# Attention scores with a second key tile for each head

## The chip, the cores and the metric

The kernel runs on one core of a Trainium2 chip. The metric is the device time of one execution in microseconds (us). TensorE is called PE, and its loads of stationary operands are shown apart as PEld; VectorE is DVE, ScalarE is ACT, GpSimd is POOL, and SyncE (SP) issues most of the DMAs.

## The reference

The program is a chain of layers over 256 latent and 256 context tokens of 1024 features: two hybrid layers (feed-forward, attention, feed-forward), then a mixer, a feed-forward, a second mixer and a last feed-forward. What the change touches is the attention of the two hybrid layers. It has 12 heads of 64 features in two groups of six; heads are handled in pairs. Cut to the scores:

```python
HEAD_DIM = 64
def gqa_attention(q, k, v):            # first group of heads
    s = einsum('bqhgd,bkhd->bhgqk', qi, k).astype(float32) * dh ** -0.5
    p = softmax(s, axis=-1)
    return einsum('bhgqk,bkhd->bqhgd', p, v)
def neighbourhood_attention(q, k, v, k_ctx, v_ctx, rpb, rows):   # second group
    s_win = einsum('bqhd,brqjhd->bhqrj', qr, kw) * scale + bias
    s_ctx = einsum('bqhd,bkhd->bhqk', qr, k_ctx) * scale
    p = softmax(concatenate([s_win, s_ctx]), axis=-1)
```

All of it is in float32. The kernel keeps that precision by splitting each operand into two float32r parts, a high part and the low rest, and by adding products of parts: high times high, high times low, low times high.

## The kernel before

A tile has 128 partitions (rows). A matmul contracts over rows, so a product with full precision takes three matmuls of 128 rows (mm3, lines 169 to 174, stationary weights, called pj where it is a projection). For scores a head has only 64 features, and the kernel packs both parts into the 128 rows. `queries` (lines 733 to 742) writes for each head a tile q[a] with the high part of the queries on the head's own 64 rows and the low part on the other 64. `keys` (lines 726 to 731) writes for a pair of heads three tiles: k[0] and k[1] hold the high part of one head's keys twice, on both halves, and k[2] holds the low parts of both heads, each on its own 64 rows. In `scores` (lines 671 to 689) each head then takes two matmuls into one PSUM bank: line 680 contracts all 128 rows of q[a] and k[a] (high times high plus low times high), and line 681 contracts only the 64 rows of the head (high times low).

Scores are taken for 128 queries at a time. In the first hybrid layer there are 6 pairs of heads by 4 tiles of queries by 2 heads, 48 in all: 24 against 512 keys, 24 (the context's queries) against 256. In the second only the latent's queries are left: 24 against 512 keys. So line 681 runs 72 times.

Around the scores: DVE takes the maximum of each row (line 685), ACT the exponents (line 687), and two steps later the generator `values` transposes the exponents on PE (line 699) and multiplies them by the values (line 708). Between these steps `fill` puts the remaining projections (the generator `others`, lines 758 to 808), three matmuls for each chunk of weights, so that PE has work while a softmax runs. Weights arrive by SP's DMAs as raw tiles; ACT writes the high part (line 115) and DVE, at a few places POOL, the low part (line 116). The order of instructions on each engine is fixed when the program is built: a scheduler places them by their dependences and by its own estimate of durations. Each engine works its list in that order. Chunk tiles (tag "ck", 54 of 128 x 512 in pool p1) are shared by the keys, queries, exponents and activations of a stage; a slot is used again when its last reader is done.

Of the kernel before, what the change touches and what calls it, by code (L numbers as in the profile page):

```python
# [6 lines left out]
F32 = mybir.dt.float32  # L7
# [8 lines left out]
# columns of the packed per-feature vectors  # L16
# [42 lines left out]
# order of the modulation's chunks: shift and scale of a norm side by side  # L59
# [7 lines left out]
class Weights:  # L67
    """Weight tiles of 128 columns in the order of use, split into two float32r parts."""
# [52 lines left out]
    def go_on(self, aside):  # L121
        """Splits on after a pause."""
        if self.held:
            self.held = False
            self.aside = aside
            while self.split_at <= min((self.pos - 1) // TPB + self.B.LOOK, self.nb - 1):
                self._split(False)
# [12 lines left out]
    def to(self, b):  # L140
        """Splits the blocks before b."""
        while self.split_at < min(b, self.nb):
            self._split()


class Builder:
# [22 lines left out]
    def mm3(self, ps, w, x, first, last):  # L169
        """Weights stationary."""  # L170
        mm = self.nc.tensor.matmul
        mm(ps, w[0], x[0], start=first, stop=False)  # L172
        mm(ps, w[0], x[1], start=False, stop=False)  # L173
        mm(ps, w[1], x[0], start=False, stop=last)  # L174

    def mm3t(self, ps, x, w, first, last):
        """Activations stationary."""
        mm = self.nc.tensor.matmul
        mm(ps, x[0], w[0], start=first, stop=False)  # L179
        mm(ps, x[0], w[1], start=False, stop=False)  # L180
        mm(ps, x[1], w[0], start=False, stop=last)  # L181
# [33 lines left out]
    def split(self, pool, src, w, tag, name, bufs=None, hi="act", lo="dve"):  # L215
        """Two float32r parts of src."""
        p = self.parts(pool, w, tag, name, bufs)
        if hi == "act":
            self.act(p[0], src)
        else:  # L220
            self.cp(p[0], src)
        (self.tt if lo == "dve" else self.gt)(p[1], src, p[0].bitcast(F32), ALU.subtract)
        return p

    def scaled(self, parts, p, scale, o):
        """Two float32r parts of p times a column."""
        self.act(parts[0][:, o], p[:, o], scale=scale)
        self.stt(parts[1][:, o], p[:, o], scale, parts[0][:, o].bitcast(F32), ALU.mult, ALU.subtract)
# [8 lines left out]
    def rstd(self, src, n, shape, bias=None):  # L237
        """1/sqrt(src/n + eps) of a small tile."""
        t = self.sml.tile(shape, F32, tag="rs%d" % shape[1], bufs=4, name="rs")
        self.act(t, src, ACTF.Sqrt, scale=1.0 / n, bias=self.eps[:shape[0], :] if bias is None else bias)  # L240
        self.nc.vector.reciprocal(t, t)
        return t

    def preload(self, func, dep):
        """Makes the scalar engine load the table of func once dep is there."""
        t = self.sml.tile([128, 1], F32, tag="pl", name="pl")
        self.act(t, dep, func, scale=0.0, bias=self.eps)
# [6 lines left out]
    def new_ss(self):  # L254
        """Place of a sum of squares."""
        return self.sml.tile([128, 1], F32, tag="ss1", bufs=16, name="ss")

    def half_bias(self, ss):
        """Half of the mean square of 1024 features, plus eps."""
        b = self.sml.tile([128, 1], F32, tag="bi", bufs=8, name="bi")  # L260
        self.ts(b, ss, 1.0 / 1024, 1e-6, ALU.mult, ALU.add)
        return b

    def rms_rows(self, h, both=False):
        """Reciprocal root mean square of 1024 features of 128 tokens, by one engine or both."""
        ss = [self.new_ss() for _ in range(2)]
        self.sq(h[:, 0:512], ss[0])
        b = self.half_bias(ss[0])
        if both:
            j = self.tmp.tile([128, 512], F32, tag="jv", bufs=1, name="jv")  # L270
            self.nc.vector.scalar_tensor_tensor(out=j, in0=h[:, 512:1024], scalar=1.0, in1=h[:, 512:1024],
                                                op0=ALU.mult, op1=ALU.mult, accum_out=ss[1])
        else:
            self.sq(h[:, 512:1024], ss[1])
        return self.rstd(ss[1], 1024.0, [128, 1], bias=b)

    def normed(self, pool, t):
        """Place of the normed rows of 128 tokens."""
# [20 lines left out]
    def pre(self, pool, T, A, shift, by=None, need=None, urgent=0):  # L299
        """Normed, scaled and transposed h: yields the 8 chunks of two parts, of by tiles of 128 tokens  # L300
        first and then of the next ones."""
# [46 lines left out]
    def follow(self, nxt):  # L348
        """The norm of layer and place nxt starts within the last product before it."""
# [6 lines left out]
    def gain_rows(self, rows):  # L356
        """Halves of gains on all partitions: [128, 2, 512]."""
# [25 lines left out]
    def out_rest(self, yg, ss, t, both):  # L383
        """Adds the normed product of 128 tokens to h."""
# [11 lines left out]
    def out_half(self, pool, ps, xs, i, G, yg, ss, tail):  # L396
        """Product of the chunks xs with half of the next weights by token; in the second half the tokens
        end one tile after the other."""
# [23 lines left out]
    def out_main(self, po, xs, n, places):  # L422
        """Product of the first chunks with the next weights, of 256 tokens; the last weights' places."""
# [13 lines left out]
    def out_tail(self, pool, po, xs, G, before=None):  # L437
        """The last 4 chunks, one tile of tokens after the other."""
# [30 lines left out]
    def halves(self):  # L469
        """Place of a block of weights in the chunks' slots."""  # L470
        return self.p1, 512, ("ck", "ck"), {}

    def fourth(self):
        """Place of a block of weights that stays until the first one of block 2's next product."""
        return self.up, TPB * 128, ("w4", "w4"), {"bufs": 2}

    def out512(self, pool, xs, G):
        """Product of the chunks xs with the next weights by token, normed and added to h."""
# [7 lines left out]
    def group(self, us, n, T, halves=False):  # L486
        """The first n products, one chunk of us after the other; their banks and the chunks."""
# [15 lines left out]
    def group256(self, us, place):  # L503
        """The first 4 products of 256 tokens, by token and one tile of tokens after the other."""
# [32 lines left out]
    def proj_tm(self, u, nt):  # L537
        """Token-major product with the next 8 groups of 4 weight tiles: one bank for each 128 tokens."""
# [8 lines left out]
    def ada_loads(self):  # L547
        """Loads the modulation's first weights and, between them, those of the first product."""
# [10 lines left out]
    def ada_pe(self, m):  # L559
        """A pair of chunks on the tensor engine, four parts of the contraction side by side."""  # L560
# [15 lines left out]
    def c_rows(self):  # L576
        """The conditions on all partitions."""
# [8 lines left out]
    def ada_dve(self, m):  # L586
        """A pair of chunks on the vector engine, columns on partitions."""
# [14 lines left out]
    def ada(self, n):  # L602
        """The next n pairs of chunks of 128 columns of the modulation's product."""
# [67 lines left out]
    def scores(self, pool, q, kz, t, bias):  # L671
        """Exponents of two heads' scores of 128 queries, and their sums."""
# [4 lines left out]
        for a in range(2):  # L677
            ps = self.psum("sc")
            o, r = slice(t * 128, (t + 1) * 128), slice(64 * a, 64 * a + 64)
            nc.tensor.matmul(ps[:, :nk], q[a][:, o], kz[a][:, k0:], start=True, stop=False)  # L680
            nc.tensor.matmul(ps[:, :nk], q[a][r, o], kz[2][r, k0:], start=False, stop=True)  # L681
# [9 lines left out]
    def values(self, pool, r, vt, vc, o):  # L691
        """Weighted values of two heads by token, in two steps."""
# [20 lines left out]
    def attn(self, l, last, end, nxt=None):  # L713
# [4 lines left out]
        if l == 0:  # L718
# [3 lines left out]
        # the first parts of each head's keys twice, and the second parts of both heads  # L722
        kz = [[pool.tile([128, 512], F32R, tag="ck", name="kz") for a in range(3)]
              for i in range(3)]

        def keys(k, x):
            for a in range(2):
# [3 lines left out]
                self.tt(k[2][r, :], x[r, :], k[a][r, :].bitcast(F32), ALU.subtract)  # L731

        def queries(x, scale=1.0):
            """Both parts of each head's queries, the first on the rows of its head."""
# [12 lines left out]
        # values, token-major  # L747
# [5 lines left out]
        # the other products run between the steps of the attention  # L753
# [60 lines left out]
        # keys and queries of the first group, normed by head and rotated  # L814
# [135 lines left out]
    def to_features(self, tms, gain, c, x, t0=0):  # L950
        """Transposes chunk c of token-major tiles to two parts, times a gain."""
# [6 lines left out]
    def decay(self, pool, X, Y, mask):  # L958
        """exp(min(X_l + Y_s, mask)) for four heads: [s, head, l]."""
# [10 lines left out]
    def log1p_exp(self, pool, x, shape):  # L970
        """log(1 + exp(-|x|))."""
# [9 lines left out]
    def mixer0(self):  # L981
        nc, tc = self.nc, self.tc
        MUL, ADD, SUB, MIN, MAX = ALU.mult, ALU.add, ALU.subtract, ALU.min, ALU.max
        with tc.tile_pool(name="mx0", bufs=1) as sp, tc.tile_pool(name="mck", bufs=16) as ck:
# [6 lines left out]
            # step sizes and gates  # L991
# [18 lines left out]
            # [t, dir, 16 + 8]  # L1010
# [20 lines left out]
            # running maxima, on rows of heads  # L1031
# [38 lines left out]
            # convolved channels: 8-11 are the groups' B and C  # L1070
# [17 lines left out]
            # keys by token of the chunk that passes a state on: dir 0 from chunk 0, dir 1 from chunk 1  # L1088
# [91 lines left out]
            # gate z, states between the chunks, and the skip  # L1180
# [208 lines left out]
    def mixer1(self):  # L1389
        nc, tc = self.nc, self.tc  # L1390
        MUL, ADD, SUB, MIN, MAX = ALU.mult, ALU.add, ALU.subtract, ALU.min, ALU.max
        with tc.tile_pool(name="mx1", bufs=1) as pool, tc.tile_pool(name="gck", bufs=16) as ck:
# [16 lines left out]
            # cumulated logarithms of the gates  # L1409
# [240 lines left out]
def weight_tiles(np, I):  # L1650
    """Tiles of 128 rows and 128 columns, in the order in which the program takes them."""
# [95 lines left out]
def host_arrays(np, I):  # L1747
# [38 lines left out]
    # rotation tables  # L1786
# [17 lines left out]
    # position bias with the window's bounds: [head, row in tile, query column, row offset, key column]  # L1804
# [44 lines left out]
```

## Time and profile before

| what | value |
|---|---|
| time, median of 3 runs | 2654.98 us (2650.44 to 2655.12) |
| span of the profiled execution | 2645.6 us; the profile gives no other time for it |
| PE busy | 2561.1 us, 97% of the span |
| DVE busy | 1749.5 us, 66% |
| ACT busy | 1157.4 us, 44% |
| POOL busy | 196.5 us, 7% |
| chain that ended last | PE 89%, DVE 6%, ACT 2% |

The span runs from the first to the last instruction of the profiled execution; the metric also counts what lies around it. Matmuls are pipelined: the record of one lasts longer than the step from its start to the next one's start. A row of PE that is fully busy is therefore not yet PE at its best pace, and the steps between starts tell the pace.

### The profile page before, as it was taken

The page shows a single profiled execution, that of the slowest core. Times are in us where ns is not written, and L with a number is a line of the kernel's source. Part 1 is how long each engine was busy: PE and PEld are TensorE (multiplying, and loading weights), DVE is VectorE, ACT ScalarE, POOL GpSimd, SP SyncE. Part 2 cuts the span into 40 slices and gives each one's busy share as a digit, 9 for nine tenths or more (in the row PEclk, how much of TensorE's full clock was granted, in tenths as well). Part 3 has the DMA queues.
Part 4 walks back from the last instruction along what each step waited for, and adds up shares of the span by engine and source line. Part 5 has one row for each costly group of instructions (what it writes and reads, how often), then busy time and mean ns, then how long its engine had stood idle before and what let it go on. Part 6 is the DMA issues. An engine that isn't in the chain of part 4 may idle for free.

```text
span 2645.6 us, 36990 instructions
## 1 busy us (share of the span) xinstructions
PE 2561.1 (97%) x13876; PEld 2142.5 (81%) x13876; DVE 1749.5 (66%) x3538; ACT 1157.4 (44%) x1994; POOL 196.5 (7%) x117
## 2 busy tenths in 40 slices
PE   6999999999999999999999999999999899999998
PEld 3888888777888887888888787997977799776997
DVE  4899435555899424898325666557767787666884
ACT  2322234444422224322224545445646566465663
POOL 2000000000000000000000101002352200121000
PEclk9999999999999999999999999999999999999999
DMA  6566331211366323565222313554434355534454
GB/s 251 183 221 220 116 122 66 72 38 58 128 222 219 102 92 104 169 220 193 96 88 86 110 62 121 185 188 151 149 128 131 108 183 184 164 123 136 147 183 157
DMA packets 124740, 375.52 MB, mean 142 GB/s; under 512 B 13840, under 2 KB 15504, under 8 KB 124304
## 3 DMA queue, kind: packets, MB, share of 16 engines
q1 hardware_dynamic: 123408, 369.22, 42.6%
q10 hardware_dynamic: 1152, 3.94, 0.4%
q8 instruction: 109, 1.79, 0.3%
q14 instruction: 71, 0.58, 0.1%
HBM read 372.05 MB, written 1.05 MB: 141 GB/s over the span
## 4 chain that ended last, share of the span: by engine, by line
PE 89%; DVE 6%; ACT 2%; issue 1%; DMA 1%; POOL 1%; SPq 0%; DVEq 0%; ACTq 0%; POOLq 0%
PE pj L172 15%; PE pj L174 15%; PE pj L173 15%; PE po L179 8%; PE po L181 8%; PE po L180 8%; PE pv L708 2%; PE tm L180 1%; PE tm L179 1%; PE tm L181 1%; PE gp L173 1%; PE gp L172 1%; PE gp L174 1%; DVE w L116 1%; PE sc L681 1%
## 5 line engine op out<-in xcount | busy, mean ns | idle before, releaser
L115 ACT ACTIVATE w<-raw 128x1024 fp32r<-128x1024 f32 (+1 forms) x564 | 572.3, 1022 | 977.1 <-PE pj L173 338.4
L116 DVE TENSOR_TENSOR w<-raw,w 128x1024 fp32r<-128x1024 f32 (+1 forms) x533 | 628.2, 1186 | 475.2 <-ACT w L115 467.8
L172 PE MATMUL pj<-uh,w 128*128 128x256 f32 (+1 forms) x2376 | 800.7, 337 | 2.1 <-ACT P L190 2.1
L174 PE MATMUL pj<-uh,w 128*128 128x256 f32 (+1 forms) x2376 | 794.2, 334 | 0.0
L173 PE MATMUL pj<-ul,w 128*128 128x256 f32 (+1 forms) x2376 | 793.7, 334 | 0.0
L172 PEld LDWEIGHTS pj<-uh,w 128*128 128x128 f32 x2376 | 451.6, 190 | 55.0 <-issue 5.3
L174 PEld LDWEIGHTS pj<-uh,w 128*128 128x128 f32 x2376 | 451.7, 190 | 48.1 <-issue 0.6
L173 PEld LDWEIGHTS pj<-ul,w 128*128 128x128 f32 x2376 | 451.8, 190 | 46.0
L597 DVE SCALAR_TENSOR_TENSOR aj<-adaw,cB 128x512 f32<-128x512 f32 x512 | 360.9, 705 | 9.5 <-DMA adaw<-in_wada 1.0
L179 PE MATMUL po<-w,sh 128*128 128x512 f32 x792 | 312.7, 395 | 0.0
L181 PE MATMUL po<-w,sl 128*128 128x512 f32 x792 | 311.9, 394 | 0.0
L180 PE MATMUL po<-w,sh 128*128 128x512 f32 x792 | 311.3, 393 | 0.0
L116 POOL TENSOR_TENSOR w<-raw,w 128x1024 fp32r<-128x1024 f32 (+1 forms) x46 | 111.6, 2425 | 1489.1 <-ACT w L115 1473.5
L181 PEld LDWEIGHTS po<-w,sl 128*128 128x128 f32 x792 | 149.0, 188 | 33.7
L179 PEld LDWEIGHTS po<-w,sh 128*128 128x128 f32 x792 | 148.9, 188 | 33.8 <-DVE yg L193 0.6
L180 PEld LDWEIGHTS po<-w,sh 128*128 128x128 f32 x792 | 148.9, 188 | 33.7 <-DVE w L116 0.7
L179 PE MATMUL tm<-w,uh 128*128 128x512 f32 x224 | 91.0, 408 | 0.0
L180 PE MATMUL tm<-w,uh 128*128 128x512 f32 x224 | 89.3, 399 | 0.6 <-POOL w L116 0.5
L193 DVE TENSOR_TENSOR sg<-sg,pj 128x512 f32<-128x512 f32 (+1 forms) x82 | 50.8, 620 | 58.1 <-PE pj L174 57.9
L181 PE MATMUL tm<-w,ul 128*128 128x512 f32 x224 | 89.1, 398 | 0.0
L190 ACT ACTIVATE ux<-tr,mod,Am 128x256 f32<-128x256 f32 (+1 forms) x96 | 49.7, 545 | 72.5 <-PE tr L327 29.2
L327 PE MATMUL tr<-cst,hn 128*128 128x128 f32 x240 | 52.4, 301 | 28.4 <-DVE hn L203 25.9
(339 smaller groups left out, 3153.2 us busy)
## 6 DMA issues: line engine op xcount, KB each, us to landing
raw<-in_w SPq DMA_DIRECT2D x554, 512.0 KB, 3.3
adaw<-in_wada SPq DMA_DIRECT2D x288, 256.0 KB, 3.2
bt<-in_bias SPq DMA_DIRECT2D x12, 192.0 KB, 2.4
hl<-in_x ACTq DMA_DIRECT2D x1, 1024.0 KB, 8.3
hc<-in_x ACTq DMA_DIRECT2D x1, 1024.0 KB, 8.6
gc<-in_gcst ACTq DMA_DIRECT2D x1, 512.0 KB, 3.6
out<-hl SPq DMA_DIRECT2D x2, 256.0 KB, 2.2
out<-hl ACTq DMA_DIRECT2D x2, 256.0 KB, 2.3
```

The costliest lines, as they stand in the source:

```text
L115: nc.scalar.activation(out=hi, in_=ri, func=ACTF.Copy)
L116: eng.tensor_tensor(out=lo, in0=ri, in1=hi.bitcast(F32), op=ALU.subtract)
L172: mm(ps, w[0], x[0], start=first, stop=False)
L173: mm(ps, w[0], x[1], start=False, stop=False)
L174: mm(ps, w[1], x[0], start=False, stop=last)
L179: mm(ps, x[0], w[0], start=first, stop=False)
L180: mm(ps, x[0], w[1], start=False, stop=False)
L181: mm(ps, x[1], w[0], start=False, stop=last)
L193: self.nc.vector.tensor_tensor(out=out, in0=a, in1=b, op=op)
L327: nc.tensor.transpose(p[:, t * 128:(t + 1) * 128], hn[t][c // 4][:, (c % 4) * 128:(c % 4 + 1) * 128], self.ident)
L597: nc.vector.scalar_tensor_tensor(out=x, in0=w, scalar=1.0, in1=self.cB[:, s, i * 512:(i + 1) * 512], op0=ALU.mult, op1=ALU.mult, accum_out ...
L708: nc.tensor.matmul(po[:, a * 64:a * 64 + 64], x[:, kt * 128:(kt + 1) * 128], vt[k0 + kt][:, vc + a * 64:vc + a * 64 + 64], start=kt == 0, ...
```

## The change

The low part of the keys gets a tile for each head: k[2] and k[3] instead of k[2] alone. Each holds the low part on the head's own 64 rows and zeros on the other 64, which six instructions on POOL for each attention write at its start. Line 681 now contracts all 128 rows: the zeros meet the low part of the queries and add nothing. The number of matmuls is the same. (The diff also takes comments and docstrings out, and the lines below 721 move down by three.)

```diff
@@ scores
-            o, r = slice(t * 128, (t + 1) * 128), slice(64 * a, 64 * a + 64)
+            o = slice(t * 128, (t + 1) * 128)
             nc.tensor.matmul(ps[:, :nk], q[a][:, o], kz[a][:, k0:], start=True, stop=False)
-            nc.tensor.matmul(ps[:, :nk], q[a][r, o], kz[2][r, k0:], start=False, stop=True)
+            nc.tensor.matmul(ps[:, :nk], q[a][:, o], kz[2 + a][:, k0:], start=False, stop=True)
@@ attn
-        kz = [[pool.tile([128, 512], F32R, tag="ck", name="kz") for a in range(3)]
+        kz = [[pool.tile([128, 512], F32R, tag="ck", name="kz") for a in range(4)]
               for i in range(3)]
+        for k in kz:
+            for a in range(2):
+                nc.gpsimd.memset(k[2 + a][64 - 64 * a:128 - 64 * a, :].bitcast(F32), 0.0)
 
         def keys(k, x):
             for a in range(2):
                 r, o = slice(64 * a, 64 * a + 64), slice(64 - 64 * a, 128 - 64 * a)
                 self.act(k[a][r, :], x[r, :])
                 self.cp(k[a][o, :], x[r, :])
-                self.tt(k[2][r, :], x[r, :], k[a][r, :].bitcast(F32), ALU.subtract)
+                self.tt(k[2 + a][r, :], x[r, :], k[a][r, :].bitcast(F32), ALU.subtract)
```

Since the two heads' low parts no longer share a tile, the scheduler also places some instructions otherwise. SP's list is unchanged, and PE's is unchanged up to the second attention. Two places follow.

On POOL, from the start of the program to the second attention; w is a block of weights, rt and qk belong to the rotation of queries and keys. Before:

```order
L113 TENSOR_TENSOR w<-raw,zero 128x1024
L116 TENSOR_TENSOR w<-raw,w 128x1024 x3
L196 TENSOR_TENSOR rt<-qk,ac 128x256 x2
L196 TENSOR_TENSOR qk<-rt 128x256 x2
L116 TENSOR_TENSOR w<-raw,w 128x1024 x6
```

And now:

```order
L113 TENSOR_TENSOR w<-raw,zero 128x1024
L116 TENSOR_TENSOR w<-raw,w 128x1024
L727 MEMSET kz 64x512 x6
L116 TENSOR_TENSOR w<-raw,w 128x1024 x2
L196 TENSOR_TENSOR rt<-qk,ac 128x256 x2
L196 TENSOR_TENSOR qk<-rt 128x256 x2
L116 TENSOR_TENSOR w<-raw,w 128x1024 x4
L727 MEMSET kz 64x512 x6
L116 TENSOR_TENSOR w<-raw,w 128x1024 x2
```

The six writes of zeros stand before the two splits of weights that POOL takes over at the start of each attention, and those splits queue behind them.

On DVE at the start of the second attention, from the keys' low parts to the first queries' low parts (qs<-qk); the first scores on PE wait for that last row. Before:

```order
L193 TENSOR_TENSOR kz<-qk,kz 64x512
L116 TENSOR_TENSOR w<-raw,w 128x1024
L241 RECIPROCAL rs<-rs 128x4
L199 SCALAR_TENSOR_TENSOR qk<-qk,g_12177,hb 128x256
L193 TENSOR_TENSOR rt<-rot,ac 128x256
L208 COPY rr<-rs 128x256
L193 TENSOR_TENSOR qk<-rt 128x256
L199 SCALAR_TENSOR_TENSOR qk<-qk,g_12177,hb 128x256
L193 TENSOR_TENSOR rt<-rot,ac 128x256
L116 TENSOR_TENSOR w<-raw,w 128x1024
L199 SCALAR_TENSOR_TENSOR qs<-qk,qs 64x256 x2
```

And now:

```order
L193 TENSOR_TENSOR kz<-qk,kz 64x512 x2
L241 RECIPROCAL rs<-rs 128x4
L199 SCALAR_TENSOR_TENSOR qk<-qk,g_12186,hb 128x256
L193 TENSOR_TENSOR rt<-rot,ac 128x256
L208 COPY rr<-rs 128x256
L116 TENSOR_TENSOR w<-raw,w 128x1024
L193 TENSOR_TENSOR qk<-rt 128x256
L199 SCALAR_TENSOR_TENSOR qk<-qk,g_12186,hb 128x256
L193 TENSOR_TENSOR rt<-rot,ac 128x256
L199 SCALAR_TENSOR_TENSOR qs<-qk,qs 64x256 x2
```

The split of weights that stood straight before qs<-qk stands four rows earlier, and a split fewer lies between the keys and the queries. On PE the sums, the transpose and the rotation that feed these rows come 14 projection matmuls earlier than before (measured on the list of PE, from 6240 to 6226), and one of the two last rotations comes one group of projections after the other.

## Rows read from the trace of the kernel before

**Rows 1.** The page's part on the chain that ended last, by engine.
```profile
PE 89%; DVE 6%; ACT 2%; issue 1%; DMA 1%; POOL 1%; SPq 0%; DVEq 0%; ACTq 0%; POOLq 0%
```

**Rows 2.** Busy time by stretch: PE, PEld, DVE, ACT, POOL, clock, DMA.
```profile
500.00:560.00 60.00, 60.00 (x308) 45.87 (x308) 32.07 (x63) 29.66 (x66) 1.68 (x1) 1.00 0.14 45
560.00:625.00 65.00, 63.53 (x371) 49.29 (x370) 40.97 (x93) 29.91 (x76) 0.00 (x0) 1.00 0.12 39
1540.00:1600.00 60.00, 58.62 (x377) 48.14 (x376) 34.51 (x72) 27.97 (x61) 0.00 (x0) 1.00 0.16 51
```

**Rows 3.** Line 681 by shape: count, busy us, mean ns, idle before.
```profile
L681 PE MATMUL sc<-kz,qs 64*128 64x512 f32 x48 | 23.5, 509 | 0.2 <-DVE kz L193 0.2
L681 PE MATMUL sc<-kz,qs 64*128 64x256 f32 x24 | 9.1, 381 | 0.0
```

**Rows 4.** Timeline of PE around one score: start, us, line, shape, count.
```profile
505.91 0.40 PE L174 MATMUL pj<-uh,w 128*128 128x512 f32 x1
506.14 0.40 PE L680 MATMUL sc<-kz,qs 128*128 128x512 f32 x1
506.47 0.50 PE L681 MATMUL sc<-kz,qs 64*128 64x512 f32 x1
506.90 0.50 PE L172 MATMUL pj<-uh,w 128*128 128x512 f32 x1
507.24 0.40 PE L173 MATMUL pj<-ul,w 128*128 128x512 f32 x1
```

**Rows 5.** The loads of the same score; in brackets the idle before.
```profile
506.47 0.18 PEld L681 LDWEIGHTS sc<-kz,qs 64*128 64x128 f32 x1 [0.37 <-issue]
506.90 0.19 PEld L172 LDWEIGHTS pj<-uh,w 128*128 128x128 f32 x1 [0.25 <-issue]
```

**Rows 6.** Timeline of PE: first and last of two scores against 256 keys.
```profile
510.65 0.28 PE L680 MATMUL sc<-kz,qs 128*128 128x256 f32 x1
...
512.13 0.39 PE L173 MATMUL pj<-ul,w 128*128 128x512 f32 x1
```

**Rows 7.** Timeline of PE at the start of the second attention.
```profile
1504.70 0.79 PE L680 MATMUL sc<-kz,qs 128*128 128x512 f32 x1 [2.05 <-DVE qs L199]
...
1507.60 0.58 PE L172 MATMUL pj<-uh,w 128*128 128x256 f32 x1
...
1511.67 0.28 PE L173 MATMUL pj<-ul,w 128*128 128x256 f32 x1
1511.79 0.28 PE L174 MATMUL pj<-uh,w 128*128 128x256 f32 x1
...
1512.28 0.40 PE L680 MATMUL sc<-kz,qs 128*128 128x512 f32 x1
...
1516.04 0.39 PE L172 MATMUL pj<-uh,w 128*128 128x256 f32 x1 [2.09 <-ACT P L190]
```

**Rows 8.** Busy time by stretch, as in rows 2: five us after that start.
```profile
1505.00:1510.00 5.00, 5.00 (x15) 3.26 (x15) 4.47 (x11) 2.38 (x6) 0.73 (x1) 0.50 0.25 92
```

**Rows 9.** Timeline of DVE and POOL at the same place.
```profile
1502.20 1.59 DVE L116 TENSOR_TENSOR w<-raw,w 128x1024 fp32r<-128x1024 f32 x1
1503.82 1.28 DVE L199 SCALAR_TENSOR_TENSOR qs<-qk,qs 64x256 fp32r<-64x256 f32 x2
1513.74 1.22 DVE L116 TENSOR_TENSOR w<-raw,w 128x1024 fp32r<-128x1024 f32 x1
1502.67 1.70 POOL L196 TENSOR_TENSOR qk<-rt 128x256 f32<-128x256 f32 x1
```

**Rows 10.** Timeline of PE near the end of the first attention's scores.
```profile
617.20 0.73 PE L680 MATMUL sc<-kz,qs 128*128 128x512 f32 x2 [0.66 <-DVE kz L208]
...
620.85 0.39 PE L680 MATMUL sc<-kz,qs 128*128 128x256 f32 x1 [0.33 <-ACT P L190]
```

**Rows 11.** Timeline: the product before the first attention ends on PE; POOL's splits.
```profile
421.58 0.40 PE L181 MATMUL po<-w,sl 128*128 128x512 f32 x1
438.54 2.38 POOL L116 TENSOR_TENSOR w<-raw,w 128x1024 fp32r<-128x1024 f32 x1 [395.05 <-ACT w L115]
1454.10 2.37 POOL L116 TENSOR_TENSOR w<-raw,w 128x1024 fp32r<-128x1024 f32 x1 [369.45 <-ACT w L115]
```

## The prediction, made before the changed kernel ran

> **What bounds the kernel now.** I read the chain that ended last first: 89% of it is PE [rows 1], so a microsecond taken from PE counts unless another engine becomes late. Next the stretches of the two attentions: PE is busy all 60 us from 500 on and 63.5 of the next 65, DVE 32.1 and 41.0 of them, ACT about half, at full clock [rows 2]. In the second attention PE is busy for 58.6 of 60 us [rows 2]. So there the order of work on PE sets the time, and the other engines have 35 to 50% of slack. Last comes the pace of PE inside these stretches, which busy time hides. The timeline shows it: from 505.91 to 506.14 an ordinary matmul of 512 columns takes a step of 0.23 us [rows 4]. Then the steps around line 681 grow: 0.33 from line 680 to line 681, 0.43 from line 681 to the next matmul, 0.34 to the one after [rows 4]. The loads tell why: the load of the 64-row operand starts only at 506.47, together with its matmul and after 0.37 us in which the loader waits for nothing but issue, and the next load, again of 128 rows, waits another 0.25 us [rows 5]. All other loads run under the matmul before them. A matmul of 64 rows between matmuls of 128 thus costs an exposed load on the way in and one on the way out.
>
> **The change, part by part.**
>
> Line 681, 72 times (48 against 512 keys, 24 against 256) [rows 3]. From 506.14 to 507.24 three steps take 1.10 us; three ordinary ones take 3 x 0.23 = 0.69 [rows 4]. The excess is 0.41 us. Against 256 keys: from 510.65 to 512.13 there are five steps (both heads' four score matmuls and one projection of 512 columns) in 1.48 us [rows 6]. At the ordinary pace of 256 columns, 0.12 us (1511.67 to 1511.79) [rows 7], and 0.23 for the projection, they would take 0.71; the excess is 0.77 for two, 0.39 each. I use 0.40 for all. With 128 rows the second score matmul looks to PE like a projection matmul, so I take the whole excess off.
>
> Where it pays: in the first attention 40 of the 48 lie in the stretch where PE never waits. The last 8 (from about 615 us) stand where PE waits for DVE's keys and for ACT's exponents to free a bank [rows 10]; what PE saves there it waits longer, so I count them at nothing. That is 40 x 0.40 = 16.0 us. In the second attention I set the first 4 apart and count the last 3, which likewise follow freshly written keys, at nothing: 17 x 0.40 = 6.8 us.
>
> The start of the second attention. PE reaches its first score early and waits 2.05 us for the queries' low parts [rows 7]; these took 1.28 us on DVE straight behind a split of 1.59 us [rows 9]. After this wait the granted clock is 0.50, that is 1.2 instead of 2.4 GHz [rows 8], and the work up to 1512.28 goes at about half pace; at 1516.04 PE waits once more, 2.09 us, for ACT's first exponents [rows 7]. The new order takes that split out from before the queries and starts the chain on PE 14 projections earlier, 14 x 0.12 = 1.7 us. I expect the first wait to go, and with it the low clock. What comes late next is the bank that ACT's first exponent frees, and it stands behind DVE's and ACT's work on the queries, which the change doesn't shorten. Bounds: the stretch from 1504.70 to 1516.04 (11.3 us) holds 8 score matmuls and 24 projections, 8 x 0.23 + 24 x 0.12 = 4.7 us at full pace, so 6.6 us and the wait of 2.05 are the most that can go, 8.7 us; at the least nothing goes, if the exponent comes no sooner. I take 4, near the middle, since the chain behind the exponent starts about 2 us sooner and PE no longer delays ACT at half pace.
>
> The zeros: six writes of 64 x 512 on POOL for each attention. The trace has no such instruction of this size. The nearest row is a split of 128 x 1024 with two inputs, 2.4 us [rows 11]; six of those would be 14.4 us. In the order they stand before POOL's two splits; they can start when the slots come free, at the latest when the product before ends on PE at 422.0, and the first split starts at 438.54 because ACT's high part comes then [rows 11]. That leaves 16.5 us, so they delay no split even at that price. What they may cost is DVE's time: a split on DVE took 1.59 us beside a POOL instruction and 1.22 without one [rows 9], 0.37 more. Twelve writes, each meeting one DVE instruction in the norm before the attention, cost at most 12 x 0.37 = 4.4 us if DVE is then always what PE waits for, and nothing if it isn't. I take 2. Three more tiles of the 54 are held; the slot waits that this brings are on instructions of the same engine that are long done. DVE's and ACT's work on the keys is the same in number and size.
>
> The sum: 16.0 + 6.8 + 4 - 2 = 24.8 us less. On the profiled execution that is 2645.6 to 2620.8 us of span. The span lies 9.4 us below the median of the runs shown, 2654.98, and I take the 9.4 to stay: 2630 us.
>
> **The rivals.**
>
> 1. The chain of the softmax comes late. With shorter steps, maxima, exponents and their copies must keep pace; DVE is 63% busy in the second half of the first attention [rows 2] and already ends PE's waits at its end [rows 10]. Then only the first half of each attention pays: 20 scores in 501 to 557 us and 6 in the second attention, 26 x 0.40 = 10.4, plus 4 and minus 2: 12.4 us less, 2643. Against it: PE never waited in that half, and the exponents have two steps of lead.
>
> 2. The exposed load isn't due to the 64 rows and stays. Then only the start and the zeros are left: 4 - 2 = 2 us less, 2653, no change that can be told. The Trainium skill speaks for it: "TensorE: Matmul & The Clock Gate", in the table on why this matters, says a single matmul over 32 rows takes the same time as one over 128, the gain of small tiles being that they run side by side; by it the padding would bring nothing. The trace disagrees on the cost in a mixed stream, 0.40 us for each [rows 4]. What stands against this rival in the rows is that ordinary matmuls of 128 rows step by 0.23, each with a new operand to load.
>
> 3. All of it pays: 72 x 0.40 = 28.8 with no loss at the ends, and the start gives its upper bound: less 28.8 + 6, about 2620.
>
> 4. Slower. The zeros stand ahead of POOL's splits of weights, and the projections' weights wait for those. If one write took longer than 16.5 / 6 = 2.75 us, every further microsecond would move the splits by 6 us in each attention, 12 in all. It outweighs 26.8 us of gain from 2.75 + 26.8 / 12 = 5.0 us for a write, twice what the largest instruction on POOL takes here [rows 11]; at 5.5 us the time would be about 2661. I know of no row that says so.
>
> **How the numbers follow.** A measurement of this kernel can tell about 0.2% (5.3 us) from no change. My forecast has a chance of 0.60, rival 1 0.18, rival 2 0.10, rival 3 0.08, rival 4 0.04. Faster by more than 0.2%: the forecast, rivals 1 and 3, and a little of rival 2, 0.88; same 0.08; slower 0.04. The range from 2619 to 2645 takes in rivals 1 and 3, the unknown of the start (0 to 8.7 us for the 4) and of the zeros (0 to 4.4 for the 2), and leaves out rivals 2 and 4.
>
> **What would show it.** In the profile after, line 681 should have 128 x 512 and 128 x 256 at about the mean of line 680, the steps around it 0.23 and 0.12 us, and no load of it should be idle for issue. The first attention, from its first score to the next product, should be 16 us shorter with PE still full. The start of the second should show a first score without a wait of 2 us and at full clock. POOL's zeros should end before ACT's high part for POOL's split. I am wrong if the steps of 0.33 and 0.43 remain, if PE shows new waits for exponents or their copies in the second half, or if the splits on POOL come late.

## The result, and the profile after

The changed kernel takes 2622.78 us (median of 4 runs, 2620.6 to 2624.53), the kernel before in the same series 2653.61 (4 runs, 2650.44 to 2655.12). The ratio is 0.9894 with an interval of 0.988 to 0.9908: between 24 and 32 us less (the two medians as they stand differ by 30.8). The forecast was 2630, its range 2619 to 2645. The profiled execution has a span of 2618.7 us (before 2645.6).

The page's first part and its chain, after. PE is 28.5 us less busy than before (2561.1), and 88% of the chain is PE where it was 89% [rows 1].

```profile
PE 2532.6 (97%) x13876; PEld 2137.4 (82%) x13876; DVE 1748.1 (67%) x3538; ACT 1156.1 (44%) x1994; POOL 203.9 (8%) x129
...
PE 88%; DVE 6%; ACT 3%; issue 1%; DMA 1%; POOL 1%; SPq 0%; DVEq 0%; ACTq 0%; POOLq 0%
```

Line 681 after, by shape (count, busy us, mean ns, idle before), the answer to [rows 3]: 128 rows now, and 0.1 us shorter each.

```profile
L681 PE MATMUL sc<-kz,qs 128*128 128x512 f32 x48 | 19.1, 404 | 0.2 <-DVE kz L193 0.2
L681 PE MATMUL sc<-kz,qs 128*128 128x256 f32 x24 | 6.9, 296 | 0.0
```

The timeline of PE around one score after, the same place as [rows 4], and behind "..." the first and last of the two scores against 256 keys, as [rows 6].

```profile
505.60 0.40 PE L680 MATMUL sc<-kz,qs 128*128 128x512 f32 x1
505.83 0.39 PE L681 MATMUL sc<-kz,qs 128*128 128x512 f32 x1
506.06 0.39 PE L172 MATMUL pj<-uh,w 128*128 128x512 f32 x1
506.29 0.40 PE L173 MATMUL pj<-ul,w 128*128 128x512 f32 x1
...
509.49 0.28 PE L680 MATMUL sc<-kz,qs 128*128 128x256 f32 x1
...
510.19 0.39 PE L173 MATMUL pj<-ul,w 128*128 128x512 f32 x1
```

From 505.60 to 506.29 the three steps take 0.69 us, where they took 1.10 [rows 4]; from 509.49 to 510.19 the five take 0.70, where they took 1.48 [rows 6]. The loads of that score, answering [rows 5], show how: each starts with the matmul before its own, 0.23 us ahead, and has no idle time in brackets.

```profile
505.60 0.19 PEld L681 LDWEIGHTS sc<-kz,qs 128*128 128x128 f32 x1
505.83 0.19 PEld L172 LDWEIGHTS pj<-uh,w 128*128 128x128 f32 x1
```

The first 60 us of the first attention, as [rows 2]: DVE and ACT work more, since more scores fall into this window, and PE stays full.

```profile
500.00:560.00 60.00, 60.00 (x355) 51.86 (x355) 38.05 (x77) 32.36 (x75) 1.69 (x1) 1.00 0.15 54
```

The first score and the 41st of 48, before, and the first after:

```profile
501.46 0.58 PE L680 MATMUL sc<-kz,qs 128*128 128x512 f32 x1
...
613.29 0.50 PE L680 MATMUL sc<-kz,qs 128*128 128x512 f32 x1 [0.48 <-DVE kz L208]
```

```profile
501.68 0.59 PE L680 MATMUL sc<-kz,qs 128*128 128x512 f32 x1
```

The end of the scores after, answering [rows 10]. The 41st now stands at 598.74, with the same idle time of 0.48; from the first score to it, 111.83 us became 97.07.

```profile
598.74 0.50 PE L680 MATMUL sc<-kz,qs 128*128 128x512 f32 x1 [0.48 <-DVE kz L208]
...
602.52 0.73 PE L680 MATMUL sc<-kz,qs 128*128 128x512 f32 x2 [0.81 <-DVE kz L208]
...
604.78 0.39 PE L680 MATMUL sc<-kz,qs 128*128 128x256 f32 x1 [0.34 <-ACT P L190]
...
606.16 0.39 PE L680 MATMUL sc<-kz,qs 128*128 128x256 f32 x1 [0.88 <-ACT P L190]
```

The start of the second attention, answering [rows 7], and the granted clock there (the number behind POOL's count), answering [rows 8].

```profile
1489.39 0.50 PE L680 MATMUL sc<-kz,qs 128*128 128x512 f32 x1 [0.39 <-DVE qs L199]
...
1498.44 0.58 PE L172 MATMUL pj<-uh,w 128*128 128x256 f32 x1 [2.35 <-ACT P L190]
1498.82 0.41 PE L173 MATMUL pj<-ul,w 128*128 128x256 f32 x1
1499.03 0.41 PE L174 MATMUL pj<-uh,w 128*128 128x256 f32 x1
```

```profile
1495.00:1500.00 5.00, 2.26 (x9) 1.86 (x10) 4.36 (x8) 4.94 (x12) 0.00 (x0) 0.74 0.30 106
1500.00:1505.00 5.00, 5.00 (x24) 4.76 (x24) 1.13 (x4) 1.94 (x5) 0.00 (x0) 0.58 0.02 3
```

The first wait fell from 2.05 to 0.39 us, and the work behind it ran at 2.4 GHz. But the wait for the bank grew to 2.35 us, and behind it the clock fell to 1.2 GHz: projections step by 0.21 us (1498.82 to 1499.03) instead of 0.12. In this execution the half clock did not go away with the first wait; it came behind the next gap.

The zeros, by their line (duration min/median/max in ns, first and last start) and in POOL's timeline the first split of weights behind them (in brackets POOL's idle time before it), answering [rows 11].

```profile
L727 POOL MEMSET kz<- x12: 517/520/522, 387.1 to 1394.6; 64x512 f32 x12
```

```profile
438.71 2.37 POOL L116 TENSOR_TENSOR w<-raw,w 128x1024 fp32r<-128x1024 f32 x1 [45.01 <-ACT w L115]
```

A write takes 0.52 us; the last of the first six ends 45.0 us before the split, which starts at 438.71 where it stood at 438.54.

### The profile page after: what moved, and what is told of

It reads as the page before. It is cut to its first block, busy times and chain, and to the rows that moved or that the text cites. A ratio compares the mean times of both kernels' runs of the same rounds, so it can differ in the third digit from the quotient of the medians.

```text
span 2618.7 us, 37016 instructions
## 1 busy us (share of the span) xinstructions
PE 2532.6 (97%) x13876; PEld 2137.4 (82%) x13876; DVE 1748.1 (67%) x3538; ACT 1156.1 (44%) x1994; POOL 203.9 (8%) x129
## 4 chain that ended last, share of the span: by engine, by line
PE 88%; DVE 6%; ACT 3%; issue 1%; DMA 1%; POOL 1%; SPq 0%; DVEq 0%; ACTq 0%; POOLq 0%
PE pj L172 15%; PE pj L173 15%; PE pj L174 15%; PE po L179 8%; PE po L181 8%; PE po L180 8%; PE pv L708 2%; PE tm L180 1%; PE tm L179 1%; PE tm L181 1%; DVE w L116 1%; PE gp L173 1%; PE gp L172 1%; PE gp L174 1%; ACT w L115 1%
```

## The experiments

Beside the first four experiments stood the kernel before with a median of 2650.98 us (17 runs), beside the last two with 2650.1 (9 runs). The profiled execution of each gives four lengths, read from starts in PE's timeline: A, the first 40 scores of the first attention (to the start of the 41st); B, from there to the next product (line 179 on och); C, the start of the second attention, from its first rotation to its 5th score; D, from there to the next product. The last column is what is left of that execution's span.

| kernel | time, us | ratio to before, interval | A | B | C | D | rest |
|---|---|---|---|---|---|---|---|
| before | 2653.61 | | 111.83 | 10.04 | 26.53 | 60.99 | 2436.2 |
| changed | 2622.78 | 0.9894, 0.988 to 0.9908 | 97.07 | 9.31 | 25.20 | 54.83 | 2432.3 |
| changed, again | 2623.77 | 0.9893, 0.988 to 0.9905 | 97.13 | 9.29 | 22.88 | 55.64 | 2435.5 |
| rows alone | 2624.4 | 0.9896, 0.9884 to 0.9909 | 97.15 | 11.42 | 25.69 | 54.44 | 2432.3 |
| zeros and tiles alone | 2649.54 | 0.9991, 0.9982 to 1.0 | 111.84 | 13.51 | 24.41 | 60.98 | 2439.1 |
| low products side by side | 2642.3 | 0.9961, 0.9949 to 0.9973 | 102.75 | 11.95 | 25.04 | 57.56 | 2443.7 |
| all scores on 64 rows | 2636.6 | 0.9946, 0.9932 to 0.996 | 100.98 | 11.80 | 23.75 | 57.21 | 2441.7 |
| Exp table early | 2622.94 | 0.9895, 0.9881 to 0.9908 | 97.09 | 9.52 | 23.12 | 54.61 | 2438.3 |

The ratios are those on record; they differ a little from the quotient of the medians shown. A and D repeat well, to 0.1 and about 1 us. B and C are disturbed by gaps and by the half clock that may follow one: with zeros and tiles alone, side by side and 64 rows, where B is above 11 us, the granted clock at its end was 0.50 over five microseconds or more; with the rows alone it was 1.00 there, and one wait for an exponent grew to 1.51 us.

**The changed kernel again.** No edit.

> The changed kernel once more, to tell what varies between two executions. First attention, from its first score to the next product: 106.4 us again, within 0.5. Time 0.988 to 0.990 of the kernel before (about 2623 us). If the 5 us by which the profiled spans differ behind the second attention belong to the change, the new span shows them again; if they are variation, points behind the second attention lie up to 5 us otherwise against the kernel before.

Measured: 2623.77 us (2622.23 to 2624.32). The first attention took 106.4 us again (A and B), and the rest of the span differs by 3.2 us between the two traces of this one kernel. The same wait for the bank, 2.36 us, stands in this trace, but the clock behind it stayed at 1.00 and projections step by 0.12 (rows of PE, and the window behind the wait).

```profile
1498.87 0.39 PE L172 MATMUL pj<-uh,w 128*128 128x256 f32 x1 [2.36 <-ACT P L190]
1499.10 0.27 PE L173 MATMUL pj<-ul,w 128*128 128x256 f32 x1
1499.21 0.28 PE L174 MATMUL pj<-uh,w 128*128 128x256 f32 x1
```

```profile
1500.00:1505.00 5.00, 5.00 (x42) 4.83 (x40) 3.26 (x7) 3.14 (x8) 0.00 (x0) 1.00 0.05 17
```

So two executions of one kernel differ in the half clock behind the same gap. From the bank's release to the 5th score the first trace took 5.29 us (1498.44 to 1503.73), this one 2.95 (1498.87 to 1501.82): the half clock cost 2.3 us here.

**The rows alone.** The kernel before with 128 rows in line 681 and its one tile of low parts; no zeros, no further tiles. It leaves out the separation of the two heads: the other head's low parts come into the sum in place of zeros.

```diff
-            nc.tensor.matmul(ps[:, :nk], q[a][r, o], kz[2][r, k0:], start=False, stop=True)
+            nc.tensor.matmul(ps[:, :nk], q[a][:, o], kz[2][:, k0:], start=False, stop=True)
```

> The kernel before with one edit: line 681 contracts 128 rows of the shared low tile, so the other head's low parts come in too; no zeros, no further tile. Theory (a 64-row matmul between 128-row ones exposes its load and the next one): the steps around line 681 fall to 0.23 and 0.12 us, the first attention shortens by 15 to 16 us, the second behind its first four scores by 6.8; 22 to 23 us less in all, 2631 us, and more if the start of the second attention gains too. Rival (the new order and the separate tiles bring the gain): no change, 2654 us.

Measured: 2624.4 us, A 97.15. The whole gain is there, without the tiles and the zeros; the time is below the 2631 expected, of which 3 us are the kernel before, whose median stands at 2650.98 here and not at 2654. Line 681 against 512 keys in this kernel:

```profile
L681 PE MATMUL sc<-kz,qs 128*128 128x512 f32 x48 | 18.6, 408 | 0.0
```

The first score of the second attention still waits here as in the kernel before, which says that this wait belongs to the order of DVE's work that the new tiles bring, and not to the rows:

```profile
1490.39 0.80 PE L680 MATMUL sc<-kz,qs 128*128 128x512 f32 x1 [2.04 <-DVE qs L199]
```

**Zeros and tiles alone.** The changed kernel, its order on each engine untouched, with line 681 on 64 rows.

```diff
-            nc.tensor.matmul(ps[:, :nk], q[a][:, o], kz[2 + a][:, k0:], start=False, stop=True)
+            nc.tensor.matmul(ps[:, :nk], q[a][64 * a:64 * a + 64, o], kz[2 + a][64 * a:64 * a + 64, k0:], start=False, stop=True)
```

> The changed kernel with line 681 back on the 64 rows of its head: the tiles, the zeros and the order of all engines are those of the changed kernel. Theory: the steps of 0.33 and 0.43 us are back, the first attention takes 121.9 us as before; what is left is the new order at the start of the second attention, 0 to 4 us less than before: 2650 to 2654. Rival (order and tiles bring the gain): 2623 us, as the changed kernel.

Measured: 2649.54 us, ratio 0.9991 (0.9982 to 1.0), 1.4 us below the kernel before. A is 111.84, as before to 0.01 us: in A 40 scores with 128 rows save 14.8 us, 0.37 each, and nothing else in the change does. PE's steps are those of [rows 4], 0.33, 0.43 and 0.34:

```profile
506.89 0.40 PE L680 MATMUL sc<-kz,qs 128*128 128x512 f32 x1
507.22 0.50 PE L681 MATMUL sc<-kz,qs 64*128 64x512 f32 x1
507.65 0.50 PE L172 MATMUL pj<-uh,w 128*128 128x512 f32 x1
507.99 0.40 PE L173 MATMUL pj<-ul,w 128*128 128x512 f32 x1
```

The first score of the second attention waits 0.39 us, as in the changed kernel, so the order alone shortens that wait.

**The two heads' low products side by side.** The kernel before, with line 680 for both heads first and then both 64-row matmuls (lines 680 and 683 of this kernel).

```diff
+        pss = [self.psum("sc") for _ in range(2)]
+        for a, ps in enumerate(pss):
             nc.tensor.matmul(ps[:, :nk], q[a][:, o], kz[a][:, k0:], start=True, stop=False)
+        for a, ps in enumerate(pss):
+            r = slice(64 * a, 64 * a + 64)
             nc.tensor.matmul(ps[:, :nk], q[a][r, o], kz[2][r, k0:], start=False, stop=True)
```

> The kernel before with both heads' line 680 first and then both heads' line 681, so that the two 64-row matmuls (rows 0 to 63, rows 64 to 127) follow each other. If what costs is the change from 128 to 64 rows and back, each pair pays once where it paid twice: half of 57 x 0.40, 11 us less (2642). If each 64-row matmul exposes its own load whatever stands beside it: no change (2654). If the two halves of the array run side by side, as the Trainium skill (TensorE: Matmul & The Clock Gate, Part 3) has it for small tiles: also the second's 0.23 or 0.12 goes, about 16 us less (2637).

Measured: 2642.3 us, A 102.75, 9.1 us less than before. The time is the one that the first theory named, but by luck; the timeline shows the third theory at work, in part of the pairs:

```profile
527.64 0.62 PE L680 MATMUL sc<-kz,qs 128*128 128x512 f32 x2
528.19 0.50 PE L683 MATMUL sc<-kz,qs 64*128 64x512 f32 x2
528.62 0.50 PE L172 MATMUL pj<-uh,w 128*128 128x512 f32 x1
528.96 0.39 PE L173 MATMUL pj<-ul,w 128*128 128x512 f32 x1
```

A row for two (x2) runs from the start of the first to the end of the second. Two matmuls of 128 rows one behind the other last 0.62; the two of 64 rows last 0.50, as long as one alone [rows 4], and the next matmul starts 0.43 us behind them, as behind one. They run at the same time, on different halves of the rows. From 527.64 to 528.96 it is 1.32 us, 0.63 more than three ordinary steps: one way in and out, 0.40, and one matmul's 0.23 for two. From the starts of line 683, 16 of the 20 pairs in A stand together like this (9 against 512 keys, 7 against 256), 25 of all 36. In the others another matmul stands between, as here:

```profile
506.74 0.50 PE L683 MATMUL sc<-kz,qs 64*128 64x512 f32 x1
507.16 0.50 PE L172 MATMUL pj<-uh,w 128*128 128x512 f32 x1
```

A pair that stands together saves one way in and out and one matmul: 9 x (0.40 + 0.23) + 7 x (0.40 + 0.12) = 9.3 us, and A fell by 9.1. By the first theory, one price saved for each of these pairs, it would be 16 x 0.40 = 6.4 us.

The Trainium skill says this in "TensorE: Matmul & The Clock Gate", in the table of the section on why this matters: the gain of few rows is that matmuls on different row groups run concurrently. The trace agrees with that half of the row: 0.50 us for two.

**All scores on 64 rows.** Line 680 too on the head's 64 rows.

```diff
-            nc.tensor.matmul(ps[:, :nk], q[a][:, o], kz[a][:, k0:], start=True, stop=False)
+            nc.tensor.matmul(ps[:, :nk], q[a][r, o], kz[a][r, k0:], start=True, stop=False)
```

> The kernel before, but line 680 too takes only the head's 64 rows (q[a][r, o] and kz[a][r, k0:]): the products of the queries' low parts with the keys' high parts are left out, and both score matmuls of a head have 64 rows. For 512 columns a head's two matmuls still stand alone between 128-row ones; for 256 columns the two heads' four stand in a row. Theory A, the price is paid where the row count changes (on the way in and on the way out) and not by every 64-row matmul: the second 64-row matmul of a head starts 0.23 us behind the first (512 columns) or 0.11 (256 columns), and the other 0.40 us stay as before; only the 24 heads with 256 columns, two by two, save one change each pair, 12 x 0.4 = 5 us, so 2643 to 2650 us against about 2651 for the kernel before. Theory B, every 64-row matmul waits for its own weight load: the second starts 0.4 us or so behind the first, 72 more exposed loads of 0.1 to 0.2 us, 2656 to 2666 us. Theory C, matmuls on the two halves of the rows run side by side: the four in a row of 256 columns take the time of two, another 12 x 0.2 = 2.6 us less, 2641 to 2647 us.

Measured: 2636.6 us (2633.34 to 2640.78), below all three ranges. The first score of two 64-row matmuls on the same half, and, behind "...", a place where both heads' four stand together:

```profile
504.94 0.40 PE L174 MATMUL pj<-uh,w 128*128 128x512 f32 x1
505.27 0.50 PE L680 MATMUL sc<-kz,qs 64*128 64x512 f32 x1
505.61 0.39 PE L681 MATMUL sc<-kz,qs 64*128 64x512 f32 x1
505.93 0.50 PE L172 MATMUL pj<-uh,w 128*128 128x512 f32 x1
506.26 0.39 PE L173 MATMUL pj<-ul,w 128*128 128x512 f32 x1
...
525.58 0.40 PE L174 MATMUL pj<-uh,w 128*128 128x512 f32 x1
525.91 0.50 PE L680 MATMUL sc<-kz,qs 64*128 64x512 f32 x2
526.24 0.40 PE L681 MATMUL sc<-kz,qs 64*128 64x512 f32 x2
526.57 0.51 PE L172 MATMUL pj<-uh,w 128*128 128x512 f32 x1
526.91 0.39 PE L173 MATMUL pj<-ul,w 128*128 128x512 f32 x1
```

From 504.94 to 506.26 four steps take 1.32 us, 0.40 more than four ordinary ones. With one 64-row matmul the excess was 0.41 [rows 4]; with two it is the same, spread over four steps instead of three. So the price belongs to the change of the row count, in and out, and not to every 64-row matmul: theory A in its mechanism, against B. The trace shows that the load doesn't run ahead across such a change, not what PE does in the pause. The Trainium skill, in "TensorEngine Tiling (Array Packing)" under Key Properties, says that changing the tiling mode drains the engine. The 0.40 us that one way in and out took here fits that. From 525.58 to 526.91 four 64-row matmuls take 0.87 us beside two ordinary steps (1.33 less 0.46): 0.40 and twice 0.23, so they ran two by two. That is theory C, at more places than I had counted, since I took only the scores against 256 keys to stand together; in A, 15 of the 20 pairs of line 680 start together and 12 of line 681. It is why the time is lower than any of the three.

**The Exp table early.** The changed kernel with one instruction more on ACT, tried as a version that might be faster still.

```diff
         sums(3)
+        self.preload(ACTF.Exp, qk[3][2][:, 0:1])
         norm(2)
```

> The changed kernel, and one more instruction on ScalarE: a one-column Exp (the kernel's own preload) behind the sums of the last query tile, so that the table for Exp is loaded before the first scores of the second attention and not between the split of the keys and the first P. In the changed kernel's traces the first P there waits behind a table load of 1.28 us, and TensorE waits 2.35 us for the P that frees its bank; in one of two traces the granted clock then fell to half for about 5 us. Theory A, the table load is on that path: the wait falls from 2.35 to about 1.1 us, the first matmul behind it starts 1 us sooner, and if the shorter gap spares the half clock, 2.4 us more come back; 1 to 4 us less than the changed kernel, 2619 to 2622 us. Theory B, the table load hides behind VectorE's own work (the maximum that P needs is late too): the wait stays at 2 us or more and the time within 1 us of the changed kernel's 2622.8 to 2623.8. Theory C, the early table load holds up ScalarE's splits of the keys, and the first scores start 1 us later: 2624 to 2626 us.

ACT's timeline in the changed kernel shows the table load ahead of the first exponents; in the experiment the exponents follow the queries' split at once, and PE's wait is 1.06 us instead of 2.35 (the changed kernel's ACT first, then the experiment's ACT and PE).

```profile
1496.31 1.28 ACT L190 ACT_TABLE_LOAD   x1
1497.61 0.69 ACT L190 ACTIVATE P<-sc,mx 128x512 f32<-128x512 f32 x1
```

```profile
1496.61 0.84 ACT L190 ACTIVATE qs<-qk 64x256 fp32r<-64x256 f32 x2
1497.47 0.69 ACT L190 ACTIVATE P<-sc,mx 128x512 f32<-128x512 f32 x1
```

```profile
1498.30 0.39 PE L172 MATMUL pj<-uh,w 128*128 128x256 f32 x1 [1.06 <-ACT P L190]
```

From the first rotation (1478.52 in the changed kernel, 1479.66 here) to the bank's release it is 18.64 us instead of 19.92: 1.3 us less, as theory A has it. The first score stands 10.9 us behind the first rotation in both, so theory C did not come. Still the time is 2622.94 us, the changed kernel's within the spread, and the half clock came here too, for some 3 us, behind a gap of 1.06. A gain of one microsecond in 2620 can't be told from none by these runs.

## Why the prediction was right, and where it wasn't

The main term, the price of a 64-row matmul, was right in its mechanism and a little too high. That the sum comes so near is partly luck: three terms set too high (the 40 scores, the start and the rest of the second attention) stand against two set too low (the last 8 and the zeros). The forecast's terms beside what the two traces of the changed kernel show (less time than before; first trace, second trace):

| term | forecast | measured |
|---|---|---|
| 40 scores of the first attention | 16.0 | 14.8, 14.7 (A) |
| its last 8 | 0 | 0.7, 0.8 (B) |
| start of the second attention | 4 | 1.3, 3.7 (C) |
| rest of the second | 6.8 | 6.2, 5.4 (D) |
| zeros | -2 | no loss seen |
| sum | 24.8 | 23.0, 24.5 (A to D) |

**The price of a 64-row matmul between 128-row ones** was read rightly from the steps, and the profile after shows what I had asked for: steps of 0.23 and 0.12, no load idle for issue, and A shorter with PE full. The size is 0.37 us for a score, not 0.40. This settles rival 2. The table row of the Trainium skill that spoke for it tells of one matmul by itself, which no run here shows, and of matmuls side by side; it says nothing on a stream that changes its row count.

**The last 8 scores** were rightly counted at about nothing. They won 0.7 us, and the waits at that end rose from 1.47 us in three [rows 10 and the 0.48 at 613.29] to 2.51 in four. Rival 1 (the softmax late in the second half) did not come: A holds scores up to 598.74 us, and PE has no idle time in it.

**The start of the second attention** is where the mechanism was wrong, in the step "I expect the first wait to go, and with it the low clock". The first wait did go (2.05 to 0.39), by the order. The low clock wasn't tied to that wait: in the first trace it came behind the next one, in the second not at all. Nor does it always follow that wait where it stays. With the low products side by side PE waits as long as before, and the granted clock over the five us behind it is 1.00 where it was 0.50 [rows 8]:

```profile
1503.27 0.50 PE L680 MATMUL sc<-kz,qs 128*128 128x512 f32 x1 [2.05 <-DVE qs L199]
```

The 4 us I took is 3.7 without it and 1.3 with it. The bank's wait, which I had named as what comes late next, did: 2.35 us.

**The zeros** cost nothing that shows. A write takes 0.52 us, not up to 2.4, and the writes ran from 387 to 394 us, as slots came free, well before the 422.0 that I took for the latest start; rival 4 needed 5 us for a write. The rows alone, with no zeros, take 2624.4 us, not less than the changed kernel.

**The level.** Of the 7.2 us by which 2630 is too high, 2.1 are in the span (2620.8 forecast, 2618.7 measured). The rest is the step "I take the 9.4 to stay": the changed kernel's median lies 4.1 us above the span of its profiled execution. Around the span lie only 1.9 us (the profiled execution with the span of 2618.7 took 2620.6, and 1.8 to 1.9 in every run after it); the other 7.5 us of the 9.4 were the difference of one execution of the kernel before from a median of three. With 17 runs its median is 2650.98, and a single execution took from 2646.32 to 2655.77.

What stays open: the spans differ by 26.9 and 25.2 us, the attentions account for 23.0 and 24.5. The remaining 3.9 and 0.7 us arise outside the attentions, where both kernels do the same work; since the two traces of one kernel differ there by 3.2, and the eight traces, whose kernels all do the same work there, by up to 11.4 (the last column of the table), they lie within the variation of executions. The medians differ by more, 30.8 and 27.2 us. The one trace of the kernel before is of an execution of some 2647.5 us (2645.6 and 1.9), below its median; whether that is all of the rest stays open.

## What to carry to other kernels

Look at steps between starts, not at busy time: PE was 97% busy before and after, and some 20 us of the gain (A and D) were hidden in steps of 0.33 and 0.43 instead of 0.23. In a stream of matmuls of 128 rows, a lone one of 64 rows took 0.37 us more here than one filled up with zeros. Filling up was the better way: two 64-row matmuls side by side still pay the way in and out, 0.63 us for the pair where two of 128 rows take 0.46. When a gain rests on a wait going away, ask which wait is next, and don't count a granted clock into the sum that the kernel doesn't set.

## What was not expected of the hardware

Two 64-row matmuls on different halves of the rows run at the same time: 0.50 us for both, where one takes 0.50, and four in 0.87 us with the way in and out. The way in and out cost 0.40 us whether one or two 64-row matmuls of a head stand between. The half clock after a gap of 2.4 us on PE came in one execution and not in another of the same kernel (0.58 against 1.00 in the same five microseconds), and cost 2.3 us there. Writing zeros of 64 x 512 on POOL takes 0.52 us.
